# Filler transposes, low parts behind their casts and moved norm transposes in layer 1's mixer, and another order of the last products

## The chip, the cores and the metric

The kernel runs on one core of a Trainium2 chip. Its engines work side by side and hand over by semaphores: TensorE (PE, with its weight loads PEld), VectorE (DVE), ScalarE (ACT), GpSimd (POOL), and SyncE (SP), which here only issues DMAs. The metric is the device time of one execution in microseconds; lower is better. Times given without a unit are microseconds from the start of the span.

## The reference

A trunk of two layers on 256 tokens of width 1024. Each layer mixes tokens, adds the result to the residual stream and normalises, then runs a product-key expert mixer (PEER) and normalises again.

```python
for i in range(DEPTH):                      # DEPTH = 2
    z = x @ w_in[i]
    hm = mlstm_mixer(...) if i % 2 == 0 else rglru_mixer(...)
    ha = cross_attention(xq, mem, xattn_w_kv[i])
    mix = jnp.concatenate([hm, ha], axis=-1) @ w_out[i]
    x = layer_norm(DN_ALPHA * x + mix, ln1_g[i], ln1_b[i])
    y = peer_ffn(x, peer_w_q[i], peer_subkeys[i], peer_u[i], peer_v[i])
    x = layer_norm(DN_ALPHA * x + y, ln2_g[i], ln2_b[i])
```

What the change touches is the end of layer 1's token mixer, an RG-LRU (a gated linear recurrence over time), and the last normalisation:

```python
a = jnp.exp(log_a)
u = jnp.sqrt(-jnp.expm1(2.0 * log_a)) * (i * xr)
h = associative_scan(a, u)                  # h[t] = a[t] * h[t-1] + u[t]
y = h * gelu(gate)                          # 768 channels; 256 more come from cross-attention
```

## The kernel before

**Products in three.** Every float32 operand of a large product is split into a high part (a rounded copy, cast by ACT in most places) and a low part (the operand less its high part, subtracted on DVE or POOL). A product is then three matmuls into one PSUM bank: high by high, high by low, low by high (`mm3`, L184 to L186). In layer 1's mixer the stationary side is the mixer's result (`mixH`, `mixL`), in the expert mixer's end the coefficients (`cH`, `cL`), and the moving side is a row block of weights (`wH`, `wL`, or the set kept longer, `eH`, `eL`).

**Weights.** `plan()` lists all row blocks in order of use. `load` issues their DMAs on SP's queue into five raw buffers, `pump(n)` casts and subtracts up to block n (by ACT's cast, or by DVE's where `cast_dve` is set, as `early(n)` does), and `next` hands out the next one. A raw buffer goes free when its block is split, and then SP can issue the next load.

**The order** is written out by hand: each engine runs its instructions in the order in which the program issues them. Generators (`norm`, `rest`, sides) are stepped by `next` between other work, so the place of a `yield` decides the place of an instruction in its engine's queue.

**The end of layer 1's mixer** (`rglru_layer`). The 768 channels are three pairs of 128 channels (b = 0, 1, 2), the 256 tokens two halves (tt = 0, 1). `over(b, tt)` issues, for one pair and one half, a multiply (L847), two scans (L849), a multiply with the gate (L851), all on DVE, and the high part's cast on ACT (L852). `low(b, tt)` subtracts the low part on DVE (L856). Between them the last row blocks of the output projection are split: the seventh by `early(7)` (cast on DVE, low part on DVE), the eighth by `pump` (cast on ACT). Then `proj_n` makes the output projection, with all eight row blocks held (`tail == DT`). `ORDER` puts the two cross-attention blocks (6, 7) first. It issues the products of the first 128 tokens (tt = 0) block by block, steps the norm, and then makes the second 128 tokens in three banks (512, 256, 256 columns): first the three blocks in the ring, for all banks, then the other five ("own"), bank by bank, with a step of the norm after each.

**The norm** (`norm`). For tt = 0: addition onto the residual (L301), statistics (L307, L309, L313), root, then scaling on ACT and POOL for the first quarter of the columns (L334, L337, L338) and on DVE for the rest (L322, L327). `turn` transposes the normalised half on PE (L348) and splits it (cast on ACT L250, low part on DVE L251) for the query projection that follows. For tt = 1 the additions follow bank by bank; `idle(n)` issues n transposes of the identity matrix that nobody reads (L247), and L422 to L428 finish the first 256 columns ahead of the query projection.

**The end of layer 1's expert mixer.** The last six row blocks are held (`late`): products of tt = 0 for both banks, then, between steps of the last norm (`last=True`), tt = 1 in three pieces. The two pieces of 256 columns lie in one PSUM bank, `y[1][1]`.

Of the kernel before, what the change touches and what calls it, by code (L numbers as in the profile page):

```python
# [7 lines left out]
F32 = mybir.dt.float32  # L8
# [10 lines left out]
P = 128  # L19
D = 1024  # L20
T = 256
DT = 8
# [11 lines left out]
EXTRA = 3  # L34
MIX_COLS = 0
GAP, GAP2 = 56, 104
FILL = (22, 5)
EXTRAS = (EXTRA, 5)
PAIRS = [list(range(8, 99, 6)), list(range(8, 105, 6))]
CLOSE = 84  # L40
# [10 lines left out]
class Trunk:  # L51
# [29 lines left out]
    def add(self, ap, n, dest=None, keep=None, cuts=1):  # L81
        self.items.append((ap, n, dest, keep, [slice(i * n // cuts, (i + 1) * n // cuts) for i in range(cuts)]))
# [67 lines left out]
    def next(self, ahead=HL_BUFS):  # L150
        while callable(self.items[self.n_got][2]) or self.items[self.n_got][3] is not None:
            self.pump(self.n_got + 1)
            self.split.pop(self.n_got, None)
            self.n_got += 1
        i = self.n_got
        if self.ahead:
            next(self.ahead, None)
        self.pump(i + ahead)
        self.n_got += 1
        self.tick()  # L160
        return self.split.pop(i)
# [37 lines left out]
    def proj_n(self, splits, stat, order=range(DT), tail=0, extra=EXTRA, hook=(-1, None)):  # L199
        sH, sL = stat  # L200
        parts = [splits, (512, 256, 256) if tail else splits]
        banks = [[self.bank() for _ in p] for p in parts]
        late = []

        def products(tt, k, late):
            t = slice(tt * P, (tt + 1) * P)
            w = parts[tt][k]
            c0 = sum(parts[tt][:k])
            for n_, dt_, (h, l) in late:
                self.mm3(banks[tt][k][:, :w], sH[:, dt_, t], sL[:, dt_, t], h[:, c0:c0 + w], l[:, c0:c0 + w],  # L210
                         n_ == 0, n_ == last[tt])
        n_ring = DT - 2 - extra
        last = (DT - 1, DT - 1 - n_ring if tail else DT - 1)
        for n, dt in enumerate(order):
            if n == hook[0]:
                hook[1]()
            late.append((n, dt, self.next(min(HL_BUFS + min(n, extra), DT - n) if tail else HL_BUFS)))
            if n + 1 > DT - tail and n + 1 < DT:
                continue
            if tail and n + 1 == DT:  # L220
                break
            for tt in range(2):
                for k in range(len(parts[tt])):
                    products(tt, k, late)
            late = []
        if not tail:
            return banks
        ln = self.norm(banks, False, True)
        if tail == DT:
            own, ring = late[2:2 + extra], late[:2] + late[2 + extra:]  # L230
            parts0 = [[c] for c in late]
        else:
            parts0 = own, ring = late[:-n_ring], late[-n_ring:]
        for part in parts0:
            for k in range(2):
                products(0, k, part)
        next(ln)
        for k in range(3):
            products(1, k, ring)
        for k in range(3):  # L240
            products(1, k, own), next(ln, None)
# [37 lines left out]
        tmp.__exit__(None, None, None)  # L279


    def norm(self, y, last, early, fill=False):
        nc, x = self.nc, self.x
        alpha = 1.0 if last or fill else ALPHA
        fine = early or last
# [2 lines left out]
        g, b = self.kept["g"], self.kept["b"]  # L288
# [6 lines left out]
        def add(tt, k):  # L295
            if fine and tt and k:
                q0, n = 1 + k, 1
            else:
                q0, n = 2 * k, 2
            xs = x[:, tt, q0 * Q:(q0 + n) * Q]  # L300
            nc.vector.scalar_tensor_tensor(xs, xs, alpha, y[tt][k][:, :n * Q], op0=ALU.mult, op1=ALU.add)  # L301
            return tt, q0, n

        def half(tt, q0, n):
            if fine and tt:
                for q in range(q0, q0 + n):
                    nc.vector.bn_stats(st[:, tt, q, :], x[:, tt, q * Q:(q + 1) * Q])  # L307
            else:
                nc.vector.bn_stats(st[:, tt, q0 // 2, :], x[:, tt, q0 * Q:(q0 + 2) * Q])  # L309
# [45 lines left out]
        if last:  # L355
            root(0)
            nc.vector.tensor_scalar(nm, mv[:, 0, 0:1], rs[:, 0:1], -1.0, op0=ALU.mult, op1=ALU.mult)
            scale_beside(0, 2)
            scale(0, 2, 2), store(nc.sync, 0, 2, 2)
            store(nc.sync, 0, 0, 2)  # L360
            yield
            half(*add(1, 0))
            yield
            half(*add(1, 1))
            yield
            half(*add(1, 2)), stats(1)
            center(1, 0, 2), root(1)
            spread(1, 0, 2), store(nc.scalar, 1, 0, 2)
            center(1, 2, 2)
            for q in (2, 3):  # L370
                spread(1, q, 1), store(nc.sync, 1, q, 1)
            return
        if fill:
            yield
            part = add(1, 0)
# [3 lines left out]
        if early:  # L379
            scale(0, 1, 1), scale(0, 2, 2)  # L380
            yield
            part = add(1, 0)
# [6 lines left out]
        self.pump(self.n_got + 3 + early)  # L389
        self.put_off = None  # L390
        self.pool_cols = MIX_COLS
        if early:
            turn(0, 0, 2), turn(0, 2, 2)
        yield
        half(*add(1, 1))
        yield
        if early:
            half(*add(1, 2))
# [21 lines left out]
        for dt in range(2):  # L420
            ds = slice(dt * P, (dt + 1) * P)
            nc.vector.scalar_tensor_tensor(x[:, 1, ds], x[:, 1, ds], rs[:, 1:2], b[:, ds], op0=ALU.mult, op1=ALU.add)  # L422
        self.idle(FILL[0])
        for dt in range(2):
# [321 lines left out]
    def rglru_layer(self):  # L746
        nc, tc, A = self.nc, self.tc, self.A
        with ExitStack() as ctx:
# [9 lines left out]
            gt = w.tile([P, 6, T], F32, name="gt")  # L758
# [55 lines left out]
            rr = w2.tile([P, 2, 6, T], F32, name="rr")  # L814
            aa = w2.tile([P, 6, T], F32, name="aa")
            th = w2.tile([P, 6, T], F32, name="th")
# [5 lines left out]
            def early(n):  # L822
                self.cast_dve = True
                self.pump(self.n_got + n)
                self.cast_dve = False
# [16 lines left out]

            def over(b, tt):
                ts, two = slice(tt * P, (tt + 1) * P), slice(2 * b, 2 * b + 2)
                nc.vector.tensor_mul(th[:, two, ts], th[:, two, ts], rr[:, 1, two, ts])  # L847
                for i in (2 * b, 2 * b + 1):
                    nc.vector.tensor_tensor_scan(aa[:, i, ts], aa[:, i, ts], th[:, i, ts],  # L849
                                                 aa[:, i, P - 1:P] if tt else 0.0, op0=ALU.mult, op1=ALU.add)  # L850
                nc.vector.tensor_mul(gt[:, two, ts], gt[:, two, ts], aa[:, two, ts])  # L851
                nc.scalar.copy(self.mixH[:, two, ts], gt[:, two, ts])  # L852

            def low(b, tt):
                ts, two = slice(tt * P, (tt + 1) * P), slice(2 * b, 2 * b + 2)
                nc.vector.tensor_sub(self.mixL[:, two, ts], gt[:, two, ts], self.mixH[:, two, ts].bitcast(F32))  # L856

            def block(co):
                cis = lambda c: [ci for ci in range(6) if any(
# [27 lines left out]
            first, last = self.xattn_out(0), self.xattn_out(1)  # L887
# [3 lines left out]
            grown(2)  # L891
            for b in range(3):
                root(b)
            over(0, 0)
            over(1, 0), low(0, 0)
            over(2, 0), low(1, 0)
            early(7)
            low(2, 0)
            self.pump(self.n_got + 8)
            over(2, 1)  # L900
            over(0, 1), low(2, 1)
            over(1, 1), low(0, 1)
            low(1, 1)
            self.proj_n((512, 512), (self.mixH, self.mixL), ORDER, DT, EXTRAS[1])


# [152 lines left out]
    def peer_layer(self, layer):  # L1059
        nc, tc, A = self.nc, self.tc, self.A  # L1060
        with ExitStack() as ctx:
# [7 lines left out]
            with ExitStack() as rctx:  # L1069
# [52 lines left out]
                for gq in range(2):  # L1122
                    qb = self.proj_t(8, (self.xH, self.xL))
                    for b in range(4):
                        o = 8 * gq + 2 * b
# [53 lines left out]
            part = lambda i: [block(i)[:, :P], block(i)[:, P:]]  # L1179
# [3 lines left out]
            th, tl = self.xHL[:, 0:3, :], self.xHL[:, 3:6, :]  # L1183
# [99 lines left out]
            y = [[self.bank() for _ in range(2)] for _ in range(2)]  # L1283
            m1, m5, m7, m6 = [self.bank() for _ in range(4)]
            late = []

            def products(tt, c0, n, part):
                t = slice(tt * P, (tt + 1) * P)
                k, o = divmod(c0, 512)
                for i_, (h, l), (cH, cL) in part:  # L1290
                    self.mm3(y[tt][k][:, o:o + n], cH[:, t], cL[:, t], h[:, c0:c0 + n], l[:, c0:c0 + n],
                             i_ == 0, i_ == P - 1)
            for i in range(P):
# [43 lines left out]
                late = []  # L1337
            self.pool_cols = MIX_COLS
            if layer:
                products(0, 0, 512, late), products(0, 512, 512, late)  # L1340
                ln = self.norm([y[0], [y[1][0], y[1][1][:, :256], y[1][1][:, 256:]]], True, False)
                next(ln), products(1, 0, 512, late)
                next(ln), products(1, 512, 256, late)
                next(ln), products(1, 768, 256, late)
                next(ln, None)
                right.close()
                return
# [9 lines left out]
            ln = self.norm(y, False, False, memory())  # L1357
# [155 lines left out]
```

## Time and profile before

| what | us |
|---|---|
| median of three runs | 1808.7 |
| the runs | 1808.12, 1808.7, 1809.78 |
| the profiled execution, its own time | 1810.35 |
| its span, first to last instruction | 1808.6 |
| layer 1's mixer end and norm | about 990 to 1023 |
| last product of the kernel to the end of the span | 1801.2 to 1808.6 |

Rows of the timeline give the start, the duration, the engine, the line, the operation with its output and inputs, and in brackets the idle time before it and what ended it. Rows of the waits give who waited for whom, the total, the number of waits and the longest. Rows of the stretches give, behind the stretch and its length, the busy time (and instructions) of PE, PEld, DVE, ACT and POOL, then the clock granted to PE, the DMA share and GB/s.

### The profile page before, as it was taken

The page shows a single profiled execution, that of the slowest core. Times are in us where ns is not written, and L with a number is a line of the kernel's source. Part 1 is how long each engine was busy: PE and PEld are TensorE (multiplying, and loading weights), DVE is VectorE, ACT ScalarE, POOL GpSimd, SP SyncE. Part 2 cuts the span into 40 slices and gives each one's busy share as a digit, 9 for nine tenths or more (in the row PEclk, how much of TensorE's full clock was granted, in tenths as well). Part 3 has the DMA queues.
Part 4 walks back from the last instruction along what each step waited for, and adds up shares of the span by engine and source line. Part 5 has one row for each costly group of instructions (what it writes and reads, how often), then busy time and mean ns, then how long its engine had stood idle before and what let it go on. Part 6 is the DMA issues. An engine that isn't in the chain of part 4 may idle for free.

```text
span 1808.6 us, 33786 instructions
## 1 busy us (share of the span) xinstructions
PE 1789.3 (99%) x12711; PEld 1649.5 (91%) x12711; DVE 1486.1 (82%) x3092; ACT 1012.1 (56%) x1785; POOL 430.4 (24%) x324
## 2 busy tenths in 40 slices
PE   8999999999999999999999999999999999999998
PEld 8999999999999888888899899999999988888886
DVE  5674669589998899998868748685999989999986
ACT  6554555455554666665657355554555456666653
POOL 2005772333332000000101368325333300000000
PEclk9999999999999999999999999999999999999999
DMA  7655566655455566665755355665545555555563
GB/s 243 207 160 190 175 186 195 193 174 164 159 160 164 190 202 210 209 201 181 257 180 179 123 176 184 195 191 187 164 163 160 160 191 202 196 194 197 195 209 128
DMA packets 95557, 334.24 MB, mean 185 GB/s; under 512 B 10652, under 2 KB 13728, under 8 KB 95136
## 3 DMA queue, kind: packets, MB, share of 16 engines
q1 hardware_dynamic: 93752, 328.93, 55.7%
q10 hardware_dynamic: 1640, 3.15, 0.5%
q8 instruction: 99, 1.62, 0.4%
q14 instruction: 66, 0.54, 0.1%
HBM read 330.98 MB, written 1.05 MB: 184 GB/s over the span
## 4 chain that ended last, share of the span: by engine, by line
PE 72%; issue 17%; POOL 8%; DVE 2%; ACT 1%; DMA 1%; POOLq 0%; DVEq 0%; SPq 0%; ACTq 0%
PE bank L186 23%; PE bank L185 23%; PE bank L184 23%; POOL wL L120 7%; PE bank L254 2%; ACT wH L110 0%; DVE wL L125 0%; DMA raw<-in_v_dram 0%; DMA raw<-in_w0kg_dram 0%; PE bank L348 0%; POOL rr L831 0%; POOL wL L123 0%; PE bank L247 0%; DVE x L301 0%; DVE x L322 0%
## 5 line engine op out<-in xcount | busy, mean ns | idle before, releaser
L110 ACT CAST wH<-raw 128x1024 fp32r<-128x1024 f32 (+3 forms) x605 | 612.2, 1013 | 670.3 <-POOL wL L120 186.3
L184 PE MATMUL bank<-xHL,wH 128*128 128x256 f32 x2536 | 715.6, 282 | 4.5 <-ACT wH L110 4.5
L186 PE MATMUL bank<-xHL,wL 128*128 128x256 f32 x2536 | 703.0, 277 | 0.7 <-DVE wL L125 0.6
L185 PE MATMUL bank<-xHL,wH 128*128 128x256 f32 x2536 | 702.6, 277 | 0.0
L125 DVE TENSOR_TENSOR wL<-raw,wH 128x1024 fp32r<-128x1024 f32 (+3 forms) x413 | 448.1, 1087 | 235.5 <-ACT wH L110 234.6
L184 PEld LDWEIGHTS bank<-xHL,wH 128*128 128x128 f32 x2536 | 477.2, 188 | 4.6 <-ACT wH L110 4.5
L186 PEld LDWEIGHTS bank<-xHL,wL 128*128 128x128 f32 x2536 | 476.8, 188 | 1.6 <-DVE wL L125 1.1
L185 PEld LDWEIGHTS bank<-xHL,wH 128*128 128x128 f32 x2536 | 477.9, 188 | 0.0
L185 PE MATMUL bank<-wL,cH 128*128 128x512 f32 x850 | 331.1, 390 | 0.9 <-DVE wL L125 0.9
L186 PE MATMUL bank<-wH,cL 128*128 128x512 f32 x850 | 330.9, 389 | 0.0
L184 PE MATMUL bank<-wH,cH 128*128 128x512 f32 x850 | 330.5, 389 | 0.0
L123 POOL TENSOR_TENSOR wL<-raw,wH 128x1024 fp32r<-128x1024 f32 (+1 forms) x121 | 256.0, 2120 | 209.9 <-ACT wH L110 209.4
L120 POOL TENSOR_TENSOR wL<-raw,wH 128x386 fp32r<-128x386 f32 x126 | 129.7, 1029 | 279.9 <-DVE wL L118 279.9
L185 PEld LDWEIGHTS bank<-wL,cH 128*128 128x128 f32 x850 | 159.5, 188 | 35.8 <-DVE wL L125 2.1
L184 PEld LDWEIGHTS bank<-wH,cH 128*128 128x128 f32 x850 | 159.6, 188 | 33.9 <-ACT cH L250 0.4
L186 PEld LDWEIGHTS bank<-wH,cL 128*128 128x128 f32 x850 | 159.6, 188 | 33.7
L1021 DVE TENSOR_TENSOR oh<-iota,i12T 128x1024 f16<-128x1024 f16 x128 | 130.3, 1018 | 0.0
L337 POOL TENSOR_TENSOR x<-x,raw 128x256 f32<-128x256 f32 x6 | 4.9, 824 | 467.0 <-ACT x L334 467.0
L118 DVE TENSOR_TENSOR wL<-raw,wH 128x640 fp32r<-128x640 f32 x126 | 104.0, 825 | 7.8 <-ACT wH L110 0.4
L1024 DVE TENSOR_TENSOR oh<-oh,gT 128x1024 f16<-128x1024 f16 x128 | 90.0, 703 | 4.4
L1154 PE MATMUL bank<-oh 128*128 128x128 f16 x1024 | 80.6, 219 | 1.1 <-DVE oh L1024 1.1
L1154 PEld LDWEIGHTS <-oh 128*128 128x128 f16 x1024 | 58.6, 97 | 6.0 <-DVE oh L1024 1.5
(336 smaller groups left out, 2121.4 us busy)
## 6 DMA issues: line engine op xcount, KB each, us to landing
raw<-in_u_dram SPq DMA_DIRECT2D x256, 512.0 KB, 3.5
raw<-in_v_dram SPq DMA_DIRECT2D x256, 512.0 KB, 4.4
raw<-in_w_q_dram SPq DMA_DIRECT2D x32, 512.0 KB, 3.8
raw<-in_w_out_dram SPq DMA_DIRECT2D x16, 512.0 KB, 3.9
raw<-in_w0qx_dram SPq DMA_DIRECT2D x8, 512.0 KB, 5.1
raw<-in_wkv_dram SPq DMA_DIRECT2D x8, 512.0 KB, 4.7
raw<-in_w0v_dram SPq DMA_DIRECT2D x8, 384.0 KB, 4.7
raw<-in_w0o_dram SPq DMA_DIRECT2D x8, 384.0 KB, 3.0
```

The lines of the kernel that those rows point to most:

```text
L110: (nc.vector.tensor_copy if self.cast_dve else nc.scalar.copy)(h[:, c], r[:, c])
L118: nc.vector.tensor_sub(l[:, k:], r[:, k:], h[:, k:].bitcast(F32))
L120: nc.gpsimd.tensor_sub(l[:, :k], r[:, :k], h[:, :k].bitcast(F32))
L123: nc.gpsimd.tensor_sub(l[:, :k], r[:, :k], h[:, :k].bitcast(F32))
L125: rest = lambda l=l, r=r, h=h, c=slice(k, n): nc.vector.tensor_sub(l[:, c], r[:, c], h[:, c].bitcast(F32))
L184: mm(out, sH, mH, start=start, stop=False, skip_group_check=True)
L185: mm(out, sH, mL, start=False, stop=False, skip_group_check=True)
L186: mm(out, sL, mH, start=False, stop=stop, skip_group_check=True)
L254: self.nc.tensor.matmul(out, lhsT, rhs, start=start, stop=stop, skip_group_check=True)
L1021: nc.vector.tensor_tensor(flat(oh[:, 1:3]), self.iota2.unsqueeze(1).to_broadcast([P, 4, P, 2]), pairs(self.i12T[:, j]), op=ALU.is_equal)
L1024: nc.vector.tensor_tensor(flat(oh[:, 0:2]), two.rearrange("p z (q e t) -> p z q e t", q=2, t=2), pairs(self.gT[:, j]), op=ALU.mult)
L1154: nc.tensor.matmul(wp[:, qs], oh[:, 2, q // 2, :, q % 2], oh[:, z, q // 2, :, q % 2], start=z == 0, stop=z == 1, skip_group_check=True)
```

## The change

Four things. (1) `proj_n` of layer 1 issues 18 transposes of the identity between the cross-attention blocks and the mixer's own. (2) In `rglru_layer` `over` no longer casts: `high` does, and `low` of a pair is issued between the two scans of the next `over`, or directly behind the cast where none follows; the seventh row block is cast on ACT, between the first half's second and third pair, and its low part moves there too; the eighth follows the third pair as before, ahead of that pair's low part. (3) The norm of layer 1's mixer issues the two `turn`s of tt = 0 one step later, behind the addition and statistics of the second bank of tt = 1. (4) At the end, tt = 0 is made for the first five of the six held blocks in both banks, and then for the sixth in both; and tt = 1 begins with the first 256 columns of the second bank, then the 512 of the first, then the last 256, with the norm's additions in that order.

```diff
-FILL = (22, 5)
+FILL = (22, 5, 18)
...
-        ln = self.norm(banks, False, True)
+        ln = self.norm(banks, False, True, turns=1 if tail == DT else 0)
...
-        for part in parts0:
+        for n, part in enumerate(parts0):
+            if tail == DT and n == 2:
+                self.idle(FILL[2])
             for k in range(2):
                 products(0, k, part)
...
-    def norm(self, y, last, early, fill=False):
+    def norm(self, y, last, early, fill=False, turns=0):
...
             yield
+            half(*add(1, 1))
+            yield
             half(*add(1, 0))
-            yield
-            half(*add(1, 1))
             yield
             half(*add(1, 2)), stats(1)
...
-        if early:
+        if early and not turns:
             turn(0, 0, 2), turn(0, 2, 2)
         yield
         half(*add(1, 1))
+        if turns:
+            turn(0, 0, 2), turn(0, 2, 2)
         yield
...
-            def over(b, tt):
-                ts, two = slice(tt * P, (tt + 1) * P), slice(2 * b, 2 * b + 2)
-                nc.vector.tensor_mul(th[:, two, ts], th[:, two, ts], rr[:, 1, two, ts])
+            half = lambda b, tt: (slice(None), slice(2 * b, 2 * b + 2), slice(tt * P, (tt + 1) * P))
+
+            def over(b, tt, before=None):
+                o = half(b, tt)
+                nc.vector.tensor_mul(th[o], th[o], rr[:, 1][o])
                 for i in (2 * b, 2 * b + 1):
+                    ts = o[2]
                     nc.vector.tensor_tensor_scan(aa[:, i, ts], aa[:, i, ts], th[:, i, ts],
                                                  aa[:, i, P - 1:P] if tt else 0.0, op0=ALU.mult, op1=ALU.add)
-                nc.vector.tensor_mul(gt[:, two, ts], gt[:, two, ts], aa[:, two, ts])
-                nc.scalar.copy(self.mixH[:, two, ts], gt[:, two, ts])
+                    if before:
+                        low(*before)
+                        before = None
+                nc.vector.tensor_mul(gt[o], gt[o], aa[o])
+
+            def high(b, tt):
+                o = half(b, tt)
+                nc.scalar.copy(self.mixH[o], gt[o])
 
             def low(b, tt):
-                ts, two = slice(tt * P, (tt + 1) * P), slice(2 * b, 2 * b + 2)
-                nc.vector.tensor_sub(self.mixL[:, two, ts], gt[:, two, ts], self.mixH[:, two, ts].bitcast(F32))
+                o = half(b, tt)
+                nc.vector.tensor_sub(self.mixL[o], gt[o], self.mixH[o].bitcast(F32))
...
-            over(0, 0)
-            over(1, 0), low(0, 0)
-            over(2, 0), low(1, 0)
-            early(7)
-            low(2, 0)
+            over(0, 0), high(0, 0)
+            over(1, 0, (0, 0))
+            self.pump(self.n_got + 7)
+            high(1, 0)
+            over(2, 0, (1, 0))
             self.pump(self.n_got + 8)
-            over(2, 1)
-            over(0, 1), low(2, 1)
-            over(1, 1), low(0, 1)
-            low(1, 1)
+            high(2, 0), low(2, 0)
+            over(2, 1), high(2, 1)
+            over(0, 1, (2, 1)), high(0, 1)
+            over(1, 1, (0, 1)), high(1, 1), low(1, 1)
...
-                products(0, 0, 512, late), products(0, 512, 512, late)
+                for part in (late[:-1], late[-1:]):
+                    products(0, 0, 512, part), products(0, 512, 512, part)
...
+                next(ln), products(1, 512, 256, late)
                 next(ln), products(1, 0, 512, late)
-                next(ln), products(1, 512, 256, late)
                 next(ln), products(1, 768, 256, late)
```

## The prediction

> **What bounds the kernel now.** I read the page's busy shares first, then the waits of PE by stretch, then the order of time on PE, DVE and ACT around the two edited places.
>
> ```profile
> PE 1789.3 (99%) x12711; PEld 1649.5 (91%) x12711; DVE 1486.1 (82%) x3092; ACT 1012.1 (56%) x1785; POOL 430.4 (24%) x324
> ...
> PE bank L184 <- ACT mixH L852: 1.9, 1, 1.9
> PE bank L186 <- DVE mixL L856: 0.7, 1, 0.7
> PE bank L348 <- POOL x L338: 0.6, 1, 0.6
> ...
> PE bank L185 <- DVE wL L125: 0.7, 2, 0.5
> PE bank L184 <- DVE x L301: 0.5, 1, 0.5
> ```
>
> PE is busy for 99% of the span, so a change can only win back PE's gaps, or what comes after its last product. The first three waits are all of PE's waits of 985 to 1060 us, which is layer 1's mixer end and its norm. The last two are from 1060 us on, and the end's own. All that the change touches is thus a few microseconds out of 1808.6.
>
> The mixer on PE, with the clock that PE was granted in one of the stretches after its gap:
>
> ```profile
> 993.53 0.39 PE L186 MATMUL bank<-wH,mixL 128*128 128x512 f32 x1
> ...
> 995.87 0.50 PE L184 MATMUL bank<-eH,mixH 128*128 128x512 f32 x1 [1.95 <-ACT mixH L852]
> ...
> 997.34 0.53 PE L186 MATMUL bank<-eH,mixL 128*128 128x512 f32 x1 [0.74 <-DVE mixL L856]
> ...
> 998.00:999.00 1.00, 1.00 (x4) 0.71 (x3) 0.96 (x4) 0.11 (x1) 0.00 (x0) 0.50 0.00 0
> ...
> 1006.55 0.39 PE L186 MATMUL bank<-wH,mixL 128*128 128x512 f32 x1
> ```
>
> PE has finished the two cross-attention rows of the output projection, waits for the first high part of the mixer, then for its low part, and then runs at a clock of 0.50 for some three microseconds. It looks like the place where the time goes. It isn't, because of what follows on DVE:
>
> ```profile
> 994.95 0.42 DVE L851 TENSOR_TENSOR gt<-gt,aa 128x256 f32<-128x256 f32 x1
> 995.29 0.42 DVE L847 TENSOR_TENSOR th<-th,rr 128x256 f32<-128x256 f32 x1
> ...
> 996.86 0.42 DVE L856 TENSOR_TENSOR mixL<-gt,mixH 128x256 fp32r<-128x256 f32 x1
> ...
> 999.10 0.69 DVE L110 CAST eH<-raw 128x1024 fp32r<-128x1024 f32 x1
> 999.83 1.23 DVE L125 TENSOR_TENSOR eL<-raw,eH 128x1024 fp32r<-128x1024 f32 x1
> ...
> 1007.51 0.42 DVE L851 TENSOR_TENSOR gt<-gt,aa 128x256 f32<-128x256 f32 x1
> 1007.85 0.98 DVE L856 TENSOR_TENSOR mixL<-gt,mixH 128x256 fp32r<-128x256 f32 x2
> 1008.75 0.68 DVE L301 SCALAR_TENSOR_TENSOR x<-x,bank 128x512 f32<-128x512 f32 x1
> ...
> 995.41 0.41 ACT L852 CAST mixH<-gt 128x256 fp32r<-128x256 f32 x1 [0.69 <-DVE gt L851]
> ...
> 999.20 1.04 ACT L110 CAST wH<-raw 128x1024 fp32r<-128x1024 f32 x1
> ```
>
> The norm's first addition (L301) needs only the products of the first half of the tokens, which end at 1006.55 + 0.39 = 1006.94. It starts at 1008.75, directly behind DVE's last low part. So DVE sets the start of the norm, with 1.8 us to spare on PE. The norm itself:
>
> ```profile
> 1014.10 1.06 POOL L338 TENSOR_TENSOR x<-x,raw 128x256 f32<-128x256 f32 x1
> ...
> 1015.21 1.20 PE L348 MATMUL bank<-ident,x 128*128 128x128 f32 x8 [0.65 <-POOL x L338]
> 1016.17 0.36 PE L184 MATMUL bank<-eH,mixH 128*128 128x256 f32 x1
> ...
> 1018.70 0.43 DVE L307 BATCH_NORM_STATS2 st<-x 128x6 f32<-128x256 f32 x1
> 1020.04 0.42 DVE L301 SCALAR_TENSOR_TENSOR x<-x,bank 128x256 f32<-128x256 f32 x1 [0.92 <-PE bank L186]
> ...
> 1021.85 0.61 DVE L422 SCALAR_TENSOR_TENSOR x<-x,rs,raw 128x128 f32<-128x128 f32 x2
> ...
> 1019.84 2.56 PE L247 MATMUL bank<-ident 128*128 128x128 f32 x22
> 1022.26 0.59 PE L425 MATMUL bank<-ident,x 128*128 128x128 f32 x2
> ...
> 1024.00:1025.00 1.00, 1.00 (x12) 1.00 (x11) 0.96 (x3) 0.40 (x1) 0.52 (x1) 1.00 0.41 123
> ```
>
> PE waits for the normalised first half (POOL ends at 1015.16), turns it with 8 transposes, and does its last products only behind these. So DVE then waits 0.92 us for PE, the only such wait of DVE here. After that L422 gives the first columns of the second half, the two transposes of L425 take them, and the query projection starts. From there to the end's products PE waits almost nowhere, so a gain at L425 should arrive whole at the end.
>
> **The change part by part.** I follow DVE, since it sets the norm, and give the shift of each event against its row above.
>
> *The row of the output weights that DVE cast* (L110 at 999.10) is now cast on ACT, whose queue is empty then: ACT ends its first high part at 995.41 + 0.41 = 995.82 and the next one can't start before 997.3, and a cast of this size takes 1.04 us there. DVE saves 999.83 - 999.10 = 0.73 us. Its low part moves ahead of the third group's scans, so the buffer goes free about 2.6 us sooner and SP issues the load that waited for it sooner; nothing is queued behind it that PE lacks.
>
> *Low parts between two scans.* The trace shows no such order. Bound from below: DVE instructions that need nothing from each other follow in 995.29 - 994.95 = 0.34 us, less than the 0.42 that one takes, and the low part costs those 0.34 wherever it stands: 0. From above: two starts behind a drained pipe instead of overlapped ones, 0.08 each, at four places: 0.6. I take 0, since a low part and the next scan share nothing. Each low part's high part is done by then (ACT needs some 0.4, the multiply and the first scan in front take 0.8).
>
> *The last pair.* Its low part (L856) stands directly behind its high part, and the other pair's low part has gone ahead of it. Before, that one lay in ACT's shadow: from the multiply at 1007.51 to the addition at 1008.75 are 1.24 us with both low parts in it. Now the same 1.24 hold one (0.42 multiply, some 0.4 for ACT, 0.34 low part and the hand-overs), and the other's 0.34 stand in front. Cost +0.34. Sum so far -0.73 + 0.34 = -0.39: the norm's first addition at 1008.36.
>
> *18 transposes in front of the mixer's rows.* L247's 22 take 1022.26 - 1019.84 = 2.42 us, 0.11 each: 18 take 1.98 us, from 993.76 (0.23 behind the start at 993.53, the step of such products) to 995.74. The first high part came at 995.87, so they end before anything needs PE, and they cost nothing. If the cover goes, by as much as they overrun. They take a bank of PSUM more, and each later tile moves on by one; the banks that come round were read well before.
>
> *What PE gains in this stretch* is the half clock and a third or so of a microsecond of waiting. At 0.50 it starts 4 products in a microsecond, where steps of 0.23 (from the end's rows, below) start more. Follow PE without that: the first low part comes 0.45 us sooner, the third group's high part about 1.4 later (still before PE asks), and its half is done at 1004.6, 2.2 sooner. The next steps keep their lengths: 4.2 for the rows in the ring (9 products of 0.23 and 18 of half the width at 0.12) and 3.4 for the first bank of the rest (15 of 0.23), so it ends at 1012.3. All of this lies under DVE's chain, whose first use of it is at 1008.36.
>
> The Trainium skill (TensorE: Matmul & The Clock Gate, "What's actually happening") says that the clock halves after an idle window of about 3.4 us and returns after a busy one. By it, fillers in the idle stretch are worth half a window, an estimate of 1.7 us; the rows show the half clock it speaks of, at a PE that was not wholly idle, but the norm didn't wait for those products.
>
> *The norm's transposes one step later.* From 1016.17 to 1019.84 PE makes 30 products, 1.8 for each bank of 15. Now it does the second bank first, until 1014.1, and then waits for POOL (1015.16 - 0.39 = 1014.77), turns (1016.17 - 1015.21 = 0.96) and does the last bank: products end at 1017.6, the 22 fillers at 1020.0. On DVE the low parts of the turned half now come behind the next addition and statistics, without a wait, since the second bank is long done. The last addition comes where its 0.92 us wait was. It could have started at 1018.70 + 0.38 = 1019.08, so 0.96 are saved: in all -0.39 - 0.96 = **-1.35**. L422 starts at 1020.5, its first result is there at about 1020.85, and PE's fillers are done 0.85 before. So DVE, not PE, sets L425. If the DVE chain were shorter than I count, PE's 1020.0 is the bound: -2.2.
>
> The end of the kernel:
>
> ```profile
> 1785.63 0.40 PE L186 MATMUL bank<-wH,cL 128*128 128x512 f32 x1
> 1785.69 1.23 DVE L125 TENSOR_TENSOR wL<-raw,wH 128x1024 fp32r<-128x1024 f32 x1 [1.26 <-ACT wH L110]
> 1786.97 0.49 PE L185 MATMUL bank<-wL,cH 128*128 128x512 f32 x1 [0.47 <-DVE wL L125]
> 1787.65 0.40 PE L184 MATMUL bank<-eH,cH 128*128 128x512 f32 x1
> 1791.82 0.40 PE L184 MATMUL bank<-eH,cH 128*128 128x512 f32 x1
> 1793.47 0.21 DVE L313 BATCH_NORM_AGGREGATE mv<-st 128x2 f32<-128x12 f32 x1
> 1797.98 0.28 PE L186 MATMUL bank<-wH,cL 128*128 128x256 f32 x1
> 1798.77 0.38 PE L184 MATMUL bank<-eH,cH 128*128 128x256 f32 x1 [0.51 <-DVE x L301]
> 1798.99 0.28 PE L185 MATMUL bank<-eL,cH 128*128 128x256 f32 x1
> 1801.20 0.42 DVE L301 SCALAR_TENSOR_TENSOR x<-x,bank 128x256 f32<-128x256 f32 x1 [2.02 <-PE bank L186]
> ```
>
> *The last weight row goes last.* From 1787.65 to 1791.82 are 18 products: 0.23 each. From 1785.63 to 1787.65 are four steps, 0.93 at that rate, and they took 2.02: the last row's late high and low parts cost 1.09. With 15 products of the other bank put between, PE asks for them about 3.5 us later, with both there: -1.09. The first half's norm now gets both banks late, at about 1790.2 and 1790.9, but its aggregate still comes some 0.5 before 1793.47.
>
> *The second half's quarter first, then the half, then the last quarter.* Both quarters lie in one bank, and PE waited at 1798.77 for the addition that reads the first of them. Steps of 0.12 would have put that product at 1798.10, and the next came 0.22 behind it: 0.67 + 0.10 = 0.77 lost. Now the 18 products of the half (4.1 us) lie between, and the addition is done before. Last product -1.09 - 0.77 = **-1.86**; DVE's statistics of the half (two like the 0.43 of L307) fit into the 2.1 us of the last quarter, so the addition at 1801.20 moves to 1799.3. What follows it (7.4 us of DVE and stores) is as before.
>
> **The sum.** -1.35 - 1.86 = -3.2 us. The profiled execution took 1810.35 us with a span of 1808.6; by it the new one takes 1807.1. The runs before lie from 1808.12 to 1809.78 with the median 1808.7, so the median forecast is **1805.5**.
>
> **Rivals.**
>
> *PE sets the query projection.* If DVE's instructions pack closer than I count, the mixer gives PE's -2.2 and the total is -4.1: 1804.6. For it: the 0.34 steps show overlap, and several of my hand-overs are copied from waits of before. Against it: DVE shows hardly a gap from 993.7 to 1018. The Trainium skill's clock rule (above) speaks for PE's side, since half a window is most of these 2.2.
>
> *The mixer gives nothing.* If the interleaving costs its upper 0.6 and the low parts of the turned half wait for ACT by as much as the 0.96 saved, only the end is left: -1.86, 1806.8. For it: POOL, ACT and DVE all hand over within a microsecond there. Against it: ACT is free for most of it.
>
> *The end's row was late only in this execution.* The change would then not do what it says there: 1.09 less, -2.1 with the rest, 1806.6. Against it: the row's load, cast and subtraction are a chain that any execution has.
>
> *Slower.* PE now idles twice within 6 us ahead of the query projection, about 0.7 us at the turn and 0.85 at L425. If this drops the clock to 0.50 as at 998, each such stretch of 3.4 us costs 1.7 of work that nothing hides, as PE is the bound there. From the second on the change is slower than before (+0.2, 1808.9), from the fifth by over 0.2%. Against it: 0.65 idle at 1015.21 and the 22 transposes behind left the clock whole (1.00 in the row of 1024), and the stretch at 998 followed some 2.7 us of waiting.
>
> **How the numbers follow.** 0.2% is 3.6 us, about what a measurement of this kernel can tell from no change, so faster begins at 1805.1. Likeliest case 0.49: its own range is 1804.5 to 1806.5, by the scatter of the runs shown, and two fifths of it lie under 1805.1. PE as the bound 0.36, nine tenths of it under. Nothing from the mixer 0.07, the end's row 0.04, slower 0.04, half of that by over 0.2%. Faster 0.49 x 0.4 + 0.36 x 0.9 = 0.52, slower 0.02, the rest the same. The range 1803.7 to 1807.2 goes from PE's bound less the runs' scatter to the case without the mixer and a little over it.
>
> **What would show it.** DVE's addition at L301 starts some 0.4 sooner, with no wait in front of the last one; PE's L425 comes some 1.35 sooner, with a gap of about 0.85 behind the fillers; the clock stays at 1.00 after the fillers; at the end PE has no wait for the last row's low part nor for the addition, and from the last product to the end are the same 7.4 us. Wrong it would be if L425 follows its fillers without a gap, if a low part between scans costs more than 0.34, or if the clock falls in the query projection.

## The result, and the profile after

The changed kernel takes 1805.91 us (median of 20 runs, 1804.9 to 1807.12), the kernel before 1808.41 on the same chip (20 runs, 1807.54 to 1810.32): a ratio of 0.9985 with a 95% interval of 0.9978 to 0.9992. The forecast was 1805.5, in a range of 1803.7 to 1807.2. The gain is about 2.5 us, or 2.7 by the ratio, against 3.2 forecast. It is under the 0.2% from which the prediction counts a kernel as faster, and to which it gave a chance of 0.52.

The profiled execution of the changed kernel has a span of 1804.7 us, 3.9 under that of before, which is more than the medians show. Where the 3.9 come from can be read at three events: the first multiply of the recurrence, the two transposes ahead of the query projection (L425, now L429), and the first product of the held rows at the end.

The row of the kernel before for the first of these, from its timeline:

```profile
993.72 0.42 DVE L847 TENSOR_TENSOR th<-th,rr 128x256 f32<-128x256 f32 x1
```

DVE's timeline of the changed kernel (the multiply is L853 here, the low part L869, the additions L303, the first scaled columns L426):

```profile
992.77 0.42 DVE L853 TENSOR_TENSOR th<-th,rr 128x256 f32<-128x256 f32 x1
...
995.13 0.40 DVE L869 TENSOR_TENSOR mixL<-gt,mixH 128x256 fp32r<-128x256 f32 x1
995.45 0.41 DVE L856 TENSOR_TENSOR_SCAN aa<-aa,th 128x128 f32<-128x128 f32 x1
...
1006.25 0.42 DVE L861 TENSOR_TENSOR gt<-gt,aa 128x256 f32<-128x256 f32 x1
1007.14 0.43 DVE L869 TENSOR_TENSOR mixL<-gt,mixH 128x256 fp32r<-128x256 f32 x1 [0.47 <-ACT mixH L865]
1007.48 0.68 DVE L303 SCALAR_TENSOR_TENSOR x<-x,bank 128x512 f32<-128x512 f32 x1
...
1017.70 0.41 DVE L303 SCALAR_TENSOR_TENSOR x<-x,bank 128x256 f32<-128x256 f32 x1
...
1019.49 0.61 DVE L426 SCALAR_TENSOR_TENSOR x<-x,rs,raw 128x128 f32<-128x128 f32 x2
```

And PE's:

```profile
992.82 2.13 PE L249 MATMUL bank<-ident 128*128 128x128 f32 x18
994.91 0.50 PE L184 MATMUL bank<-eH,mixH 128*128 128x512 f32 x1
...
1013.93 1.20 PE L350 MATMUL bank<-ident,x 128*128 128x128 f32 x8 [0.59 <-POOL x L340]
...
1016.77 2.56 PE L249 MATMUL bank<-ident 128*128 128x128 f32 x22
1019.90 0.59 PE L429 MATMUL bank<-ident,x 128*128 128x128 f32 x2 [0.56 <-DVE x L426]
```

The multiply is 0.95 us sooner than before, and everything ahead of it is code that the change doesn't touch: over the 14 profiles here it lies between 992.36 and 994.14, for old and new mixers alike. So these 0.95 us are scatter and no gain. From it to the transposes the kernel before takes 1022.26 - 993.72 = 28.54 us, the changed one 1019.90 - 992.77 = 27.13: **1.41 from the mixer**. The bracket in the row of L429 names the bound: PE is done with its 22 fillers and waits 0.56 us for DVE, and DVE's last addition at 1017.70 has no wait in front of it any more.

The stretch from 984 to 1030 us in the changed kernel (busy times of the five engines, PE's clock, DMA share, GB/s):

```profile
984.00:1030.00 46.00, 44.81 (x291) 39.54 (x290) 41.54 (x83) 21.94 (x39) 16.44 (x27) 1.00 0.30 95
```

and in the kernel before:

```profile
984.00:1030.00 46.00, 42.63 (x257) 37.05 (x256) 42.62 (x84) 21.56 (x40) 15.37 (x26) 0.96 0.28 88
```

The clock is whole now (1.00, where it was 0.96). What this is worth can't be read from these rows; the experiments show it.

The end of the changed kernel, PE's timeline:

```profile
1780.34 0.39 PE L184 MATMUL bank<-eH,cH 128*128 128x512 f32 x1
...
1794.74 0.40 PE L186 MATMUL bank<-wH,cL 128*128 128x512 f32 x1
1794.97 0.28 PE L184 MATMUL bank<-eH,cH 128*128 128x256 f32 x1
...
1796.98 0.28 PE L186 MATMUL bank<-wH,cL 128*128 128x256 f32 x1
```

and DVE's:

```profile
1790.94 0.21 DVE L315 BATCH_NORM_AGGREGATE mv<-st 128x2 f32<-128x12 f32 x1
...
1793.29 0.41 DVE L303 SCALAR_TENSOR_TENSOR x<-x,bank 128x256 f32<-128x256 f32 x1
...
1797.30 0.42 DVE L303 SCALAR_TENSOR_TENSOR x<-x,bank 128x256 f32<-128x256 f32 x1 [0.65 <-PE bank L186]
```

PE has no gap. The addition that it used to wait for is done at 1793.70, before the quarter that shares its bank begins at 1794.97. From the first product of the held rows to the last addition are 1797.30 - 1780.34 = 16.96 us, where the kernel before took 1801.20 - 1782.40 = 18.80: 1.84 in this pair of executions. From the last addition to the end of the span are 7.4 us in both. So 3.9 = 0.95 (ahead of the change) + 1.41 + 1.84, less 0.30 in the 760 us between.

### The profile page after: what moved, and what is told of

It is laid out like the page before. It is cut to its first block, busy times and chain, and to the rows that moved or that the text cites. A ratio compares the mean times of both kernels' runs of the same rounds, so it can differ in the third digit from the quotient of the medians.

```text
span 1804.7 us, 33822 instructions
## 1 busy us (share of the span) xinstructions
PE 1788.4 (99%) x12729; PEld 1649.6 (91%) x12729; DVE 1486.7 (82%) x3091; ACT 1012.9 (56%) x1786; POOL 430.0 (24%) x324
## 4 chain that ended last, share of the span: by engine, by line
PE 72%; issue 16%; POOL 7%; DVE 3%; ACT 1%; DMA 1%; POOLq 0%; SPq 0%; DVEq 0%
PE bank L186 23%; PE bank L185 23%; PE bank L184 23%; POOL wL L120 7%; PE bank L256 3%; ACT wH L110 0%; DVE wL L125 0%; DMA raw<-in_w0kg_dram 0%; DVE x L303 0%; DVE aa L856 0%; DVE x L324 0%; POOL wL L123 0%; DVE st L309 0%; DVE x L329 0%; PE bank L350 0%
```

## The experiments

Each experiment ran 11 times with a profile of one execution; the kernel before ran 33 times beside each batch of four (medians 1808.95, 1808.49 and 1808.87). "Mixer" is the time from the first multiply to the transposes (L425 or its like), "end" from the first product of the held rows to the last addition, both from the profile.

| kernel | median us | ratio to before, 95% interval | mixer us | end us |
|---|---|---|---|---|
| before | 1808.41 | 1 | 28.54 | 18.80 |
| changed | 1805.91 | 0.9985 [0.9978, 0.9992] | 27.13 | 16.96 |
| mixer_only | 1807.36 | 0.9989 [0.9980, 0.9998] | 27.14 | 17.69 |
| end_only | 1807.54 | 0.9993 [0.9984, 1.0002] | 28.87 | 16.95 |
| no_fill | 1806.86 | 0.9987 [0.9978, 0.9996] | 27.14 | 16.96 |
| turns_back | 1807.71 | 0.9996 [0.9987, 1.0005] | 28.20 | 16.96 |
| fill_only | 1808.08 | 0.9998 [0.9989, 1.0007] | 28.51 | 17.68 |
| dve_cast | 1806.69 | 0.9991 [0.9982, 1.0000] | 27.89 | 16.95 |
| low_behind | 1805.87 | 0.9984 [0.9975, 0.9993] | 26.83 | 16.95 |
| low_in_norm | 1805.13 | 0.9982 [0.9973, 0.9991] | 26.48 | 16.96 |
| quarter_only | 1807.59 | 0.9994 [0.9985, 1.0003] | 28.52 | 16.92 |
| row_only | 1808.06 | 0.9996 [0.9987, 1.0005] | 28.53 | 17.73 |
| after_again | 1806.19 | 0.9986 [0.9977, 0.9995] | 27.15 | 16.95 |
| low_in_norm2 | 1805.44 | 0.9980 [0.9971, 0.9989] | 26.48 | 16.96 |

The intervals of the ratios are as wide as most of the effects, so the two columns on the right tell more than the medians. They repeat to some 0.03 us where the code is the same, but for two executions that are explained below: the end of the kernel before (18.80, a late weight row) and the mixer of end_only (28.87, a longer stretch at half clock).

**The two places apart.**

- mixer_only: the changed kernel with the end's products and additions in the old order.
- end_only: the kernel before with the end's products and additions in the new order.

> The mixer's three parts alone, the end as before. My theory: DVE's chain sets the query projection, which starts 1.35 us sooner, so about 1.35 under the kernel before (ratio 0.9993), and the profile shows 0.5 to 0.9 of idle PE in front of L429. Rival, PE sets it (half clock and all): 2.2 under. Rival, the mixer gives nothing: 0. The profile also shows the old end a second time: if the last row's load is late only now and then, PE's waits for its low part differ from the 1.09 us of the kernel before.

> The end's two reorderings alone, the mixer as before. My theory: 1.09 for the last row and 0.77 for the two quarters, 1.86 under the kernel before (ratio 0.9990). Rival, the row was late only in the execution that was profiled: about 0.8 under.

The mixer alone gives its 1.40 with 0.58 us of idle PE in front of L429, as forecast, and not PE's 2.2. The end is another matter. In mixer_only, with the old end, PE's waits from 1770 us on are these and no more:

```profile
PE bank L184 <- DVE x L303: 0.5, 1, 0.5
```

The wait for the last row's low part is gone, though the old order of products is there: the end takes 17.69 and not 18.80. The weight row was late in the one execution that the prediction had to go by. In end_only it was late again, as ACT's timeline shows:

```profile
1784.20 1.05 ACT L110 CAST wH<-raw 128x1024 fp32r<-128x1024 f32 x1 [3.33 <-DMA raw<-in_v_dram]
```

It is cast 2.99 us behind the first held product (1781.21), later than in the kernel before (1784.61 - 1782.40 = 2.21), and the new order hides it whole: 16.95. The median of end_only is 1.41 us under the kernel before, between the 1.86 expected and the 0.8 of the rival, and its interval (0.9984 to 1.0002) holds both.

**Is it the clock?** The fillers are taken out of the changed kernel, and put alone into the kernel before.

```diff
no_fill, from the changed kernel
-                self.idle(FILL[2])
fill_only, from the kernel before
+FILL = (22, 5, 18)
...
+            if tail == DT and n == 2:
+                self.idle(FILL[2])
```

> The changed kernel without the 18 filler transposes. My theory: PE idles some 2 us, may fall to the half clock for one window, but DVE's chain does not move (its additions at L303 at the same distance from the scans), PE has about 0.6 to spare in front of L429: 0 to 0.4 over the changed kernel. Rival, the fillers' rule by itself (half of a 3.4 us window): 1.7 over the changed kernel.

> The kernel before with the 18 filler transposes and nothing else. My theory: the clock stays at 1.00, PE ends the first half's products up to 2 us sooner, and nothing moves behind it, since DVE sets the norm: from the first multiply behind the roots (L847) to L425 28.5 us as in the kernel before, the time 0 to 0.3 under it. Rival, the clock's half window is worth its whole 1.7: 1.7 under, 26.8 us between these two.

In fill_only the clock is whole from 990 to 1005 us:

```profile
990.00:1005.00 15.00, 14.26 (x71) 11.56 (x70) 14.54 (x32) 6.33 (x12) 0.00 (x0) 1.00 0.22 65
```

and what PE has won there it loses again in a longer wait some 18 us later, in PE's timeline of the same kernel:

```profile
1014.19 1.21 PE L350 MATMUL bank<-ident,x 128*128 128x128 f32 x8 [2.21 <-POOL x L340]
```

The 0.65 us of waiting at the norm's transposes in the kernel before have become 2.21, and the mixer still takes 28.51 us. The rival of a half window, 1.7 us, is out by these spans: repairing PE's clock alone buys nothing here, because DVE and POOL decide when the transposes can start. The mixer of no_fill is 27.14, equal to that of the changed kernel, but its clock stayed whole without fillers (1.00 from 984 to 1030, with 1.95 us of idle PE), so this run doesn't show what the changed kernel would lose at half clock. Its median lies 0.7 to 1.0 above that of the changed kernel, where 0 to 0.4 was expected, but it was measured in another batch, and the intervals hold both; whether some of its executions pay for a half clock stays open. That the clock isn't quite free in the old order is shown by end_only, which has the old mixer:

```profile
984.00:1030.00 46.00, 43.27 (x259) 37.91 (x258) 42.06 (x83) 20.51 (x36) 14.92 (x27) 0.93 0.27 87
```

That is (1 - 0.93) x 46 = 3.2 us lost clock, twice that of before, and the mixer takes 28.87, that is 0.33 more. With a second such stretch PE is late for the transposes: L348 starts at 1014.34 with no wait for POOL in front of it, and what DVE hid before no longer fits.

**The place of the norm's transposes.**

```diff
-        ln = self.norm(banks, False, True, turns=1 if tail == DT else 0)
+        ln = self.norm(banks, False, True, turns=0)
```

> The changed kernel with the norm's transposes where they were, ahead of the second bank. My theory: PE waits for POOL some 2.4 us from the end of the first bank, then turns and makes two banks, so the last addition waits for PE again and the 22 fillers end about 0.9 after L429's data: 0.9 over the changed kernel. Rival, the move is worth nothing because DVE sets everything: 0.

PE's timeline of turns_back:

```profile
1013.67 1.21 PE L350 MATMUL bank<-ident,x 128*128 128x128 f32 x8 [2.39 <-POOL x L340]
1018.32 2.56 PE L249 MATMUL bank<-ident 128*128 128x128 f32 x22
1020.73 0.59 PE L429 MATMUL bank<-ident,x 128*128 128x128 f32 x2
```

The wait is the 2.4 us forecast, the fillers follow the late products, and L429 follows the fillers without a gap: here PE sets the query projection. The mixer takes 28.20, 1.07 more than the changed kernel, where 0.9 was expected. So of the 1.41, about 1.1 is lost when the move of the transposes is taken out. The move was not tried by itself in the kernel before, so how much of this it gives without the other parts is not shown.

**DVE's chain.** Two edits that lengthen or shorten it by a counted amount, and a third for a version that is better than both.

```diff
dve_cast, from the changed kernel
-            self.pump(self.n_got + 7)
+            early(7)
low_behind, from the changed kernel
-            over(1, 1, (0, 1)), high(1, 1), low(1, 1)
+            over(1, 1), high(1, 1), low(0, 1), low(1, 1)
low_in_norm, from the changed kernel; in norm, between() is low(1, 1)
-            over(1, 1, (0, 1)), high(1, 1), low(1, 1)
+            over(1, 1), high(1, 1), low(0, 1)
...
-        half(*add(0, 0)), half(*add(0, 1)), stats(0)
+        part = add(0, 0)
+        between()
+        half(*part), half(*add(0, 1)), stats(0)
```

> The changed kernel with the seventh row's cast back on DVE. My theory: DVE's chain is 0.73 us longer, so 27.86 instead of 27.13 from the first multiply to L429, and 0.7 over the changed kernel. Rival, DVE has slack here: 0.

> The changed kernel with the low part of (0, 1) behind over(1, 1) again, where it lies in ACT's shadow. My theory: DVE's 0.47 of waiting for the last high part shrinks to about 0.14 and the norm comes 0.33 sooner: 26.8 us from the first multiply to L429, 0.3 under the changed kernel. Rival, low parts between scans are cheaper there: 0 or over it.

> As low_behind, and the last low part of all goes behind the norm's first addition, which doesn't need it. My theory: DVE has no wait at all there and the gap in front of the statistics is filled too: 0.64 under the changed kernel, 26.5 us from the first multiply to L429, with PE's gap in front of L429 still over 0. Rival, PE needs the last low part sooner (it is read at about 9.4 us behind the norm's start of products) and waits: 0.2 or less under.

The mixer took 27.89, 26.83 and 26.48 us, where 27.86, 26.8 and 26.5 were expected: each edit of DVE's chain moved L429 by the amount counted, to within 0.03 us. In DVE's timeline of low_in_norm the wait for ACT is gone:

```profile
1006.02 0.42 DVE L872 TENSOR_TENSOR mixL<-gt,mixH 128x256 fp32r<-128x256 f32 x1
1006.36 0.68 DVE L303 SCALAR_TENSOR_TENSOR x<-x,bank 128x512 f32<-128x512 f32 x1
1006.96 0.42 DVE L872 TENSOR_TENSOR mixL<-gt,mixH 128x256 fp32r<-128x256 f32 x1
1007.29 0.69 DVE L311 BATCH_NORM_STATS2 st<-x 128x6 f32<-128x512 f32 x1
```

One low part lies in the shadow of the last cast, the other between the norm's first addition and its statistics. The placement that low_behind undoes is thus the one part of the change that was found to cost time: 27.13 - 26.83 = 0.30 us.

**The end's parts, and the versions once more on one chip.**

- quarter_only: the kernel before with only the new order of the second half's three pieces.
- row_only: the kernel before with only the last held row's products last.
- after_again, low_in_norm2: unchanged copies of the changed kernel and of low_in_norm.

> The kernel before with the other order of the second half's three pieces, and nothing else. My theory: 0.73 from the first product of the held rows (17.7 to 16.95, or 18.8 to 18.07 where the last row is late), 0.7 under the kernel before. Rival, the wait for the bank only moves to another addition: 0.

> The kernel before with the last held row's products last, and nothing else. My theory: 17.69 from the first product of the held rows to the last addition, whether the row is late or not; under the kernel before by 1.1 times the share of executions in which it is late, which two profiles of three with the old order put at about a third: 0.4. Rival, late in every execution: 1.1 under. Rival, late only once: 0.

> The changed kernel once more, beside the others on one chip: 1.41 from the mixer, 0.73 from the pieces and 0 to 1.1 from the last row, 2.1 to 3.2 under the kernel before, 27.13 us from the first multiply to L429 and 16.95 at the end.

> The version with the last low part behind the norm's first addition once more, beside the changed kernel: 0.65 under the changed kernel, 26.48 us from the first multiply to L429. Rival, its lower time was the chip's: equal to the changed kernel.

quarter_only ends in 16.92 us, with the old order of rows and no wait on PE from 1770 us on: the pieces give 17.69 - 16.92 = 0.77 where the row is in time. row_only ends in 17.73, as mixer_only does without a late row (17.69), though its own row was cast 1.69 behind the first held product: the new order hid the lateness. Up to the lateness that the kernel before could bear (2.21 - 1.09 = 1.12) the order of rows doesn't matter; three of the 14 profiles were later than that, before, end_only and row_only. The load itself is issued 4.15 or 4.16 us ahead of the first held product in all 14, and lands 4.1 us (low_in_norm) to 7.1 us (end_only) after its issue. So what varies is the landing, and not when the load is issued. The three late ones have the old mixer, as have fill_only and quarter_only, which were not late, and none of the nine with the new mixer was late. Whether that is chance or something of the new mixer is open. The measured medians (1.28 and 0.81 under before) lie above what one profile of each explains, and within their intervals.

low_in_norm2 is 0.75 under after_again by the medians of one chip, as in the profile (27.15 - 26.48 = 0.67). It is the fastest version here, 0.9980 [0.9971, 0.9989] of the kernel before.

## Why the prediction was right, and where a size was off

**What bounds the mixer** was right: DVE's chain, with PE's gap and half clock hidden under it. fill_only shows it directly, and L429 moved with each counted edit of DVE.

**Its terms.** The cast taken off DVE: 0.73 forecast, 27.89 - 27.13 = 0.76 measured. The low parts between scans: 0 taken, out of 0 to 0.6; the next scan starts 995.45 - 995.13 = 0.32 us behind the low part, less than its own 0.40, so 0 was right. The last pair: 0.34 lost forecast, 0.30 measured by undoing it. The norm's first addition came 15.03 - 14.71 = 0.32 sooner counted from the first multiply, where 0.39 was forecast; the last one 26.32 - 24.93 = 1.39, where 1.35 was. So the part between the two additions, which the move of the transposes was to shorten by 0.96, gave 1.39 - 0.32 = 1.07, the same 1.07 that turns_back loses. The sum of -1.35 was -1.41, and the two transposes waited 0.56 for DVE where 0.85 was forecast.

**The 18 fillers** end as the first high part arrives, and cost nothing: the first product that needs it starts 994.91 - 992.77 = 2.14 us behind the first multiply, as in no_fill (995.55 - 993.41).

**The end's pieces.** 0.77 forecast, 0.73 to 0.77 measured.

**The last row** is the term that was mis-sized. It was put at 1.09 and its rival, that it was late only in this execution, at a chance of 0.04, with the argument that its load, cast and subtraction are a chain that any execution has. The step that failed is this argument: the chain is there in each execution, but the time of its load's landing is not the same. The cast came between 0.20 and 2.99 us behind the first held product, and only a lateness beyond 1.12 would make PE wait. Of the old order's profiles one in four (before; not mixer_only, fill_only, quarter_only) had the wait. With no such wait the sum is 1.41 + 0.75 = 2.2, with one in every execution 3.3, and the two measured gains, 2.5 and 2.7, lie between.

**Luck in the number.** The gain was 0.7 us short of the forecast, and the time only 0.4 off: the forecast started from 1808.7, the median of three runs, and the median of 20 is 1808.41. The 0.3 between them offset a part of the error.

**The rivals.** PE as the bound of the query projection was given 0.36, too much: with the transposes moved, DVE is the bound in all eight profiles, and PE is it only where they stay in their old place (turns_back). The clock that falls ahead of the query projection: it stayed whole there in all profiles of the changed kernel.

## What to carry to other kernels

A gap and a low clock on the busiest engine are worth nothing until one has followed what its next consumer waits for; here the consumer was late on DVE by itself, and the repaired clock only turned into a longer wait some 18 us later. A wait that ends on a DMA must be read in more than one execution before its length goes into a sum: here the steps that hang on engines alone repeated to a few hundredths of a microsecond where the clock was the same, and this wait came and went. And where an engine is the bound, look for instructions of the next stage that are ready already, to put into its waits for another engine: that gave low_in_norm its 0.65 us.

## What the runs showed of the hardware that was not expected

The granted clock fell to 0.50 for 3.41 us in the old mixer of before, quarter_only and row_only, for 6.83 us in that of end_only, and, with 1.95 us of idle PE in the same place, not at all in no_fill. The second wait of 0.7 us, which the old mixer has behind the first one and no_fill has not, is not the reason: in row_only the clock is down before that wait begins. PE's timeline of row_only, and the clock there:

```profile
994.65 0.57 PE L184 MATMUL bank<-eH,mixH 128*128 128x512 f32 x1 [1.96 <-ACT mixH L852]
996.12 0.80 PE L186 MATMUL bank<-eH,mixL 128*128 128x512 f32 x1 [0.48 <-DVE mixL L856]
...
994.50:994.75 0.25, 0.10 (x1) 0.10 (x1) 0.22 (x1) 0.10 (x1) 0.00 (x0) 1.00 0.00 0
994.75:995.00 0.25, 0.25 (x1) 0.20 (x2) 0.25 (x2) 0.00 (x0) 0.00 (x0) 0.87 0.00 0
995.00:995.25 0.25, 0.25 (x2) 0.00 (x0) 0.25 (x1) 0.00 (x0) 0.00 (x0) 0.50 0.00 0
```

The length of an idle stretch doesn't decide by itself either: turns_back has one of 2.39 us, and its clock is 1.00 from 984 to 1030.

What the traces show instead is a grid in time. In every profile the clock also falls behind the kernel's last product. In the four profiles that have a fall in the mixer too, the two falls are 805.55 us (before, end_only, quarter_only) or 808.96 us (row_only) apart, which is 236 or 237 times 3.413 us. If the falls lie on such a grid throughout, the fall at the end places it in all 14 profiles. PE's idle time can then be counted for each interval of the grid, around the mixer and at the end. Every interval that ends in a fall holds about 1.95 us or more of it (row_only's mixer 1.95, end_only's 2.02), and none that the clock came through whole holds more than 1.88. The 2.39 us of turns_back lie across a grid line, 1.19 and 1.20, and no_fill has 0.29 us of its stretch ahead of a line and 1.66 behind it. By this count no_fill was spared by the place of the grid, and another execution of it might not be. The Trainium skill (TensorE: Matmul & The Clock Gate, "What's actually happening") says that the clock falls after an idle window of 3413 ns that runs free of the kernel. The length of the stretches agrees, once and twice that window, and so does the grid; that PE must be idle for a whole window does not, since it made products within each of the four that ended in a fall in the mixer.

Transposes that nobody reads keep the clock whole: in no_fill PE has 3.88 us, from 1017.56 to 1021.44, with nothing but transposes and 0.58 us of idling, at a clock of 1.00.

A load's time to landing is not steady even at the same place: the last row blocks' loads took 3.3 to 6.3 us in the kernel before and 3.6 to 5.3 in the changed one, together with the two rows of the norm that are issued right behind them.
